# Attention's scale of q: sums of squares as rows through memory instead of columns straight from TensorE

## The chip, the cores and the metric

The kernel runs on one core of one Trainium2 chip. The metric is the device time of one execution in microseconds (us), as the median of several. Five engines work side by side: TensorE (PE, with its weight loads as PEld), VectorE (DVE), ScalarE (ACT), GpSimd (POOL) and SyncE (SP), which here issues all DMAs.

## The reference

A network of four layers over 16 meta tokens and 1024 tokens of width 1024, batch 1, fp32: sliding-window attention, mLSTM, HGRN2, attention again. Every layer adds its branch to x. What the change touches is the norm of q, and of k, ahead of the scores (16 heads of 64 for q, 4 for k):

```python
def rmsnorm(x, g):
    xf = x.astype(jnp.float32)
    y = xf * lax.rsqrt(jnp.mean(xf * xf, axis=-1, keepdims=True) + EPS)
    return (y * g.astype(jnp.float32)).astype(x.dtype)
...
def attention_branch(u, w_in, q_gain, k_gain, sinks, w_out, valid, pos):
    q, k, v, z = _split(u @ w_in, (A_W, A_KVW, A_KVW, A_W))
    q = rope(rmsnorm(q.reshape(bsz, lp, A_HEADS, A_HD), q_gain), pos)
    k = rope(rmsnorm(k.reshape(bsz, lp, A_KV, A_HD), k_gain), pos)
    ...
    o = sliding_window_attention(q, k, v, sinks, valid)
    return (o * jax.nn.silu(z.astype(jnp.float32))).astype(u.dtype) @ w_out
```

The window is 128 tokens; a softmax with one sink per head closes the scores.

## The kernel before

Activations lie transposed: features on the 128 partitions, tokens along the free axis. The 1040 tokens form chunks of 400, 384 and 256 columns (384, 384 and 256 for q, z and the output of the last layer, which needs no meta tokens there). Blocks of tokens are 16 (the meta tokens, block 0) and then 128 each; chunk 0 has blocks 0 to 3, chunk 1 has 4 to 6, chunk 2 has 7 and 8. Large products are split into high and low parts and made as three products each (`uh,wh`, `ul,wh`, `uh,wl`, line 232, eight feature tiles to an output tile). A weight tile arrives as two raw halves (`wr`, L208; two raw buffers in all), is cast on ACT (`wh`, L196), and DVE takes the difference (`wl`, L197).

**q.** The 16 heads of q make eight tiles t of 128 features, two heads to a tile. For each tile and chunk n the product is brought from PSUM by ACT twice (L576 with the gain, L577 squared, `sq`, one of six temporary tiles `t`). Then come steps at set delays behind the projection, in ns of PE's planned time (`D_Q` = 2000, 3000, 4000, 6000; `D_Q0` for the first two tiles of the first layer):

- `factors`: the load of the cosines and sines of a chunk (`cs`, L586, one buffer);
- `stat_q` (L590 to L610): sums of squares of each token and head. For every block one product (L599) with the block of squares as weights (128 × 128) and two mask columns as the moving side, so that the sums come out as two columns per block, with tokens on the partitions. In the first layer DVE adds the row's epsilon column (L604) and ACT makes Ln (L607) and Exp (L610); in the last layer ACT makes Ln from PSUM (L609) and Exp. The result is the tile `rq`, 1/rms of each token and head as columns, 128 × 2 per block;
- `rope` (L626 to L628), on q itself and on a copy of it with halves exchanged, which four DMAs bring (L570, issued as soon as q is out of PSUM);
- the split of q into high and low (`qs`, L528 and L529).

The scale is not put on q. The score step `S_step` takes it: PE makes the scores of two tiles (`pm`, L728 and L729), DVE multiplies by `rq`, masks and takes the minimum in one operation (L736), ACT makes Exp with the sum (L739), DVE the reciprocal (L741), POOL the product with it (L742). Then PE transposes (L757), ACT and DVE split (L759, L760), and PE multiplies by v (L775).

k's norm has its own step (`stat`, L616 a product with a 128-column mask as weights). The mLSTM layer writes rows of its gates to memory (`rowsd`, L927) and reads them back (`rw`, L992).

**Order.** PE's order is written by hand: a list of steps, each with a planned cost, woven by shares (`weave`) with events put in at their delays (`spread`, `chain`). The planned cost of a step moves the steps behind it against others; PE then runs in that order. ACT, DVE, POOL and SP are ordered by the tile scheduler. SP runs its DMAs in program order: one that waits holds all behind it.

Of the kernel before, what the change touches and what calls it, by code (L numbers as in the profile page):

```python
# [9 lines left out]
F32 = mybir.dt.float32  # L10
F32R = mybir.dt.float32r
AF = mybir.ActivationFunctionType
ALU = mybir.AluOpType
PSUM = bass.MemoryType.PSUM

P = 128
D = 1024
KT = D // P
NMETA = 16
# [7 lines left out]
CHUNK_BLOCKS = [(0, 1, 2, 3), (4, 5, 6), (7, 8)]  # L27


def blk(b):  # L30
    return (0, NMETA) if b == 0 else (NMETA + P * (b - 1), P)
# [24 lines left out]
MM = 1.0 / 2.4  # L56
# [58 lines left out]
def hybrid_kernel(ctx: ExitStack, tc: tile.TileContext, ins, out, layers=(0, 1, 2, 3)):  # L115
    nc = tc.nc
    v, s, g, pe, sp = nc.vector, nc.scalar, nc.gpsimd, nc.tensor, nc.sync
# [6 lines left out]
    dram = ctx.enter_context(tc.tile_pool(name="dram", bufs=1, space=bass.MemoryType.DRAM))  # L124
# [4 lines left out]
    def nm(x):  # L129
        ctr[0] += 1  # L130
        return f"{x}{ctr[0]}"
# [16 lines left out]
    def psum(tag, bufs):  # L148
        return ps.tile([P, 512], F32, tag="p", name=nm(tag), bufs=8)
# [4 lines left out]
    def psa():  # L154
        return psum("pa", 1)
# [8 lines left out]
    eps, one = consts[:, 0:1], consts[:, 1:2]  # L164
# [316 lines left out]
    def layer_a(i, j, first, last, fin, scale=None):  # L481
        win, wout = ins["a_win"][j], ins["a_wout"][j]
        chunks = LAST_CHUNKS if last else CHUNKS
        R = {}
# [72 lines left out]
        def qk_proj(src, gcol, work, fsplit, ch, t=None, fetched=False):  # L557
# [23 lines left out]
            def finish(n, c0, cn):  # L581
# [7 lines left out]
                def stat_q():  # L589

                    sq = late[n][1]
                    nb = len(CHUNK_BLOCKS[n])
                    R["rq", t, n] = rq = R["mix"].tile([P, 2 * nb], F32, tag=f"rq{n}", name=nm("rq"), bufs=4)
                    st = psa()
                    for k, b in enumerate(CHUNK_BLOCKS[n]):
                        if last and b == 0:
                            continue
                        q0 = blk(b)[0] - c0
                        pe.matmul(st[:, 2 * k : 2 * k + 2], sq[:, q0 : q0 + P], R["masks"][:, 0:P:64], start=True, stop=True)  # L599
                    z = slice(2 if last and n == 0 else 0, 2 * nb)  # L600
                    if first:
                        b0 = CHUNK_BLOCKS[n][0]
                        e = scale.ecol[:, b0 : b0 + nb].rearrange("p (k c) -> p k c", c=1).to_broadcast([P, nb, 2])
                        v.scalar_tensor_tensor(rq.rearrange("p (k c) -> p k c", c=2),  # L604
                                               st[:, z].rearrange("p (k c) -> p k c", c=2), 1.0 / 64, e,
                                               op0=ALU.mult, op1=ALU.add)
                        s.activation(rq, rq, AF.Ln)  # L607
                    else:
                        s.activation(rq[:, z], st[:, z], AF.Ln, bias=eps, scale=1.0 / 64)  # L609
                    s.activation(rq[:, z], rq[:, z], AF.Exp, scale=-0.5)  # L610

                def stat():
                    factors()
# [18 lines left out]
                turn = fsplit(lambda: late[n][0], n, c0, cn)  # L632
                if t is not None:
                    d = D_Q0 if first and t < 2 else D_Q
                    return [(d[0], [0.0, factors, None]), (d[1], [108 * len(CHUNK_BLOCKS[n]), stat_q, None]),
                            (d[2], [0.0, rope, None]), (d[3], turn)]
                d = D_K1 if fetched else D_K0 if scaled else D_K
                return [(d[0], [(8 if scaled else 4) * cn * MM, stat, None]), (d[1], [0.0, rope, None]), (d[2], turn)]

# [216 lines left out]
        for i in range(3, 12):  # L856
            for t in (2 * (i // 3), 2 * (i // 3) + 1):
                at = [id(z) for z in body]
                q, k = (at.index(id(z)) if id(z) in at else -1
                        for z in (order["q", t, i % 3], order["S", i // 3 - 1, i % 3]))  # L860
# [663 lines left out]
    for pos, i in enumerate(layers):  # L1524
# [16 lines left out]
        if tail is not None:  # L1541
            oa0, ob0 = tail
            first, seq = outs([oa0[0], ob0[0], oa0[1], oa0[2], ob0[1], ob0[2]])
# [6 lines left out]
            for n, start, end in ((2, t_b, t_b + h0 + h1), (1, t_a, t_b + h0), (0, 0.0, t_b)):  # L1550
                d, share = NORM_AT[n]
# [17 lines left out]
    first, seq = outs(tail[0] + tail[1])  # L1569
# [12 lines left out]
    ahead, k = 0.0, 0  # L1582
# [120 lines left out]
```

## Time and profile before

| | |
|---|---|
| time, median of 3 runs | 2576.55 us (2576.28 to 2578.90) |
| profiled execution | 2579.45 us, span 2577.7 us |
| granted clock, mean | 0.997 |
| first attention layer's mixers | about 22 to 488 us of the span |
| mLSTM and HGRN2 layers | about 488 to 2125 us |
| last attention layer's mixers | about 2125 to 2522 us |
| `stat_q` steps | 48 (24 in each attention layer) |
| products on L599 | 136 (two passes each) |

In a row of the trace, the first two numbers are its start from the start of the span and its duration (us); then engine, line, operation, what is written and read, and shapes. Idle time of the engine just ahead of it stands in brackets, with what ended it. A group of rows by line gives the least, median and largest duration in ns. PE's matmuls overlap: a product's duration is longer than the pitch from one to the next.

### The profile page before, as it was taken

The page shows a single profiled execution, that of the slowest core. Times are in us where ns is not written, and L with a number is a line of the kernel's source. Part 1 is how long each engine was busy: PE and PEld are TensorE (multiplying, and loading weights), DVE is VectorE, ACT ScalarE, POOL GpSimd, SP SyncE. Part 2 cuts the span into 40 slices and gives each one's busy share as a digit, 9 for nine tenths or more (in the row PEclk, how much of TensorE's full clock was granted, in tenths as well). Part 3 has the DMA queues.
Part 4 walks back from the last instruction along what each step waited for, and adds up shares of the span by engine and source line. Part 5 has one row for each costly group of instructions (what it writes and reads, how often), then busy time and mean ns, then how long its engine had stood idle before and what let it go on. Part 6 is the DMA issues. An engine that isn't in the chain of part 4 may idle for free. (4 is left out here: it accounts for less than half of the span.)

```text
span 2577.7 us, 55464 instructions
## 1 busy us (share of the span) xinstructions
PE 2530.0 (98%) x20614; PEld 2481.4 (96%) x20614; DVE 2028.8 (79%) x5602; ACT 1748.3 (68%) x4699; POOL 248.8 (10%) x572
## 2 busy tenths in 40 slices
PE   9999999999999999999999999999999999999999
PEld 8898989999999999999999999999999998999999
DVE  7896898786767676767676788988878988887896
ACT  8866766576565656565675758877676857867772
POOL 0321231000000000000000000110010000321320
PEclk9999999999999999999999999999999999999999
DMA  5223212022232212121221111111111013212112
GB/s 156 65 66 86 58 54 70 25 58 50 50 47 53 46 46 51 48 48 51 48 53 52 55 44 34 35 35 35 43 34 40 29 52 93 65 47 78 56 42 78
DMA packets 103345, 140.27 MB, mean 54 GB/s; under 512 B 15370, under 2 KB 58515, under 8 KB 103075
## 3 DMA queue, kind: packets, MB, share of 16 engines
q1 hardware_dynamic: 103074, 136.73, 19.7%
q8 instruction: 162, 2.65, 0.4%
q14 instruction: 109, 0.88, 0.1%
HBM read 121.83 MB, written 4.27 MB: 49 GB/s over the span
## 5 line engine op out<-in xcount | busy, mean ns | idle before, releaser
L232 PE MATMUL pj<-uh,wh 128*128 128x384 f32 (+2 forms) x2688 | 903.2, 336 | 6.7 <-ACT uh L402 6.2
L232 PE MATMUL pj<-ul,wh 128*128 128x384 f32 (+2 forms) x2688 | 864.8, 322 | 0.3
L232 PE MATMUL pj<-uh,wl 128*128 128x384 f32 (+2 forms) x2688 | 864.3, 322 | 0.0
L232 PEld LDWEIGHTS pj<-uh,wh 128*128 128x128 f32 x2688 | 507.9, 189 | 14.8 <-ACT uh L402 6.2
L232 PEld LDWEIGHTS pj<-ul,wh 128*128 128x128 f32 x2688 | 508.5, 189 | 4.7 <-DVE ul L197 0.9
L232 PEld LDWEIGHTS pj<-uh,wl 128*128 128x128 f32 x2688 | 507.5, 189 | 0.0
L197 DVE TENSOR_TENSOR wl<-wr,wh 128x512 fp32r<-128x512 f32 (+1 forms) x338 | 233.3, 702 | 74.6 <-ACT wh L196 71.3
L196 ACT CAST wh<-wr 128x512 fp32r<-128x512 f32 (+1 forms) x338 | 203.6, 613 | 93.5 <-PE pj L327 31.7
L327 PE MATMUL pj<-yh,wh 128*128 128x384 f32 (+2 forms) x768 | 252.9, 329 | 10.1 <-DVE x L330 8.3
L330 DVE TENSOR_TENSOR x<-x,pj 128x384 f32<-128x384 f32 (+2 forms) x480 | 233.8, 507 | 34.5 <-PE pj L327 33.2
L327 PE MATMUL pj<-yh,wl 128*128 128x384 f32 (+2 forms) x768 | 245.9, 320 | 0.0
L327 PE MATMUL pj<-yl,wh 128*128 128x384 f32 (+2 forms) x768 | 245.8, 320 | 0.0
L282 PE MATMUL pj<-wh,uh 128*128 128x256 f32 (+1 forms) x768 | 221.9, 289 | 0.0
L282 PE MATMUL pj<-wl,uh 128*128 128x256 f32 (+1 forms) x768 | 216.2, 282 | 0.0
L282 PE MATMUL pj<-wh,ul 128*128 128x256 f32 (+1 forms) x768 | 215.7, 281 | 0.0
L739 ACT ACTIVATE Sm<-Sm,s 128x257 f32<-128x257 f32 (+2 forms) x272 | 131.1, 483 | 88.9 <-DVE s L736 86.0
L742 POOL TENSOR_TENSOR Sm<-Sm,s 128x512 f32<-128x512 f32 (+2 forms) x136 | 139.3, 1025 | 402.5 <-DVE s L741 381.1
L459 ACT ACTIVATE t<-t 128x384 f32<-128x384 f32 (+2 forms) x240 | 118.2, 492 | 67.6 <-DVE t L458 65.8
L196 ACT CAST yh<-r 128x384 fp32r<-128x384 f32 (+2 forms) x120 | 56.8, 479 | 151.1 <-PE pj L327 135.6
L327 PEld LDWEIGHTS pj<-yh,wh 128*128 128x128 f32 x768 | 144.5, 188 | 14.3 <-DVE x L330 10.4
L282 PEld LDWEIGHTS pj<-wh,uh 128*128 128x128 f32 x768 | 144.6, 188 | 0.6
L282 PEld LDWEIGHTS pj<-wl,uh 128*128 128x128 f32 x768 | 144.8, 189 | 0.3
(332 smaller groups left out, 5684.2 us busy)
## 6 DMA issues: line engine op xcount, KB each, us to landing
wr<-in_b_win SPq DMA_DIRECT2D x124, 256.0 KB, 2.9
wr<-in_a_win SPq DMA_DIRECT2D x80, 256.0 KB, 2.8
wr<-in_c_win SPq DMA_DIRECT2D x64, 256.0 KB, 2.8
wr<-in_a_wout SPq DMA_DIRECT2D x32, 256.0 KB, 2.9
rw<-rowsd SPq DMA_DIRECT2D x64, 128.0 KB, 4.4
wr<-in_b_wout SPq DMA_DIRECT2D x32, 256.0 KB, 2.8
t<-t SPq DMA_DIRECT2D x100, 48.0 KB, 1.9
cs<-in_rope SPq DMA_DIRECT2D x11, 400.0 KB, 3.3
```

The costliest lines, as they stand in the source:

```text
L196: s.copy(h, src)
L197: v.tensor_tensor(l, src, h.bitcast(F32), op=ALU.subtract)
L232: pe.matmul(acc[:, :cn], a[:, k, :], b[:, k, c0 : c0 + cn], start=(k == 0 and i == 0), stop=(k == KT - 1 and i == 2))
L282: pe.matmul(acc[:cn, :nc], a[:, k, c0 : c0 + cn], m[:, kk, :], start=(k == 0 and j == 0), stop=(k == KT - 1 and j == 2))
L327: pe.matmul(acc[:, :cn], a[:, k, mc], b, start=(k == 0 and i == 0), stop=(k == 1 and i == 2))
L330: v.tensor_tensor(x[:, m, c0 : c0 + cn], x[:, m, c0 : c0 + cn], acc[:, :cn], op=ALU.add)
L459: s.activation(a[:, :cn], a[:, :cn], AF.Exp)
L739: s.activation(Sm[:nq, u, : nk + 1], Sm[:nq, u, : nk + 1], AF.Exp, scale=-1.0, bias=st[:nq, u : u + 1], accum_out=den[:nq, u : u + 1])
L742: g.tensor_tensor(Sm[:nq, :, :nk], Sm[:nq, :, :nk], den[:nq].rearrange("p (u c) -> p u c", c=1).to_broadcast([nq, 2, nk]), op=ALU.mult)
```

## The change

`stat_q` is cut in two. The first step makes one product for the whole chunk, with the two mask columns as weights (128 × 2) and all squares of the chunk as the moving side; ACT brings the two rows of sums out of PSUM (the scaled sums in the first layer, their Ln in the last) into the first two partitions of the tile of squares, and SP writes them to memory (`sd`). The second step, `rows_q`, comes behind `rope`, at least 1700 ns of planned time after the first: two DMAs (one a head) read the rows back as columns of `rq`, 4 bytes a piece, and for chunk 0 of the first layer a small third one the meta tokens, after POOL has set those columns to 1. DVE's addition and ACT's Ln (first layer) and Exp (both) are made on the columns as before. In all there are 48 writes and 104 reads more. The planned cost of the step goes from 108 ns a block (432, 324, 216) to 4 × columns / 2.4 (667, 640, 427).

```diff
@@ -589,25 +589,39 @@
                 def stat_q():
 
                     sq = late[n][1]
+                    st = psa()
+                    pe.matmul(st[:2, :cn], R["masks"][:, 0:P:64], sq, start=True, stop=True)
+                    if first:
+                        s.activation(sq[0:2], st[:2, :cn], AF.Identity, scale=1.0 / 64)
+                    else:
+                        s.activation(sq[0:2], st[:2, :cn], AF.Ln, bias=eps[0:2], scale=1.0 / 64)
+                    R["sd", t, n] = dram.tile([2, cn], F32, name=nm("sd"))
+                    sp.dma_start(R["sd", t, n], sq[0:2])
+
+                def rows_q():
+
                     nb = len(CHUNK_BLOCKS[n])
                     R["rq", t, n] = rq = R["mix"].tile([P, 2 * nb], F32, tag=f"rq{n}", name=nm("rq"), bufs=4)
-                    st = psa()
-                    for k, b in enumerate(CHUNK_BLOCKS[n]):
-                        if last and b == 0:
-                            continue
-                        q0 = blk(b)[0] - c0
-                        pe.matmul(st[:, 2 * k : 2 * k + 2], sq[:, q0 : q0 + P], R["masks"][:, 0:P:64], start=True, stop=True)
-                    z = slice(2 if last and n == 0 else 0, 2 * nb)
+                    d = R["sd", t, n]
+                    k = 0
+                    if n == 0:
+                        k = 1
+                        if not last:
+                            g.memset(rq[:, 0:2], 1.0)
+                            with nc.allow_non_contiguous_dma(reason="scale of each row"):
+                                sp.dma_start(rq[:NMETA, 0:2], d[:, :NMETA].rearrange("h t -> t h"))
+                    o = blk(CHUNK_BLOCKS[n][k])[0] - c0
+                    with nc.allow_non_contiguous_dma(reason="scale of each row"):
+                        for hh in range(2):
+                            sp.dma_start(rq[:, 2 * k + hh :: 2], d[hh, o:cn].rearrange("(k t) -> t k", t=P))
+                    z = rq[:, 2 if last and n == 0 else 0 :]
                     if first:
                         b0 = CHUNK_BLOCKS[n][0]
                         e = scale.ecol[:, b0 : b0 + nb].rearrange("p (k c) -> p k c", c=1).to_broadcast([P, nb, 2])
-                        v.scalar_tensor_tensor(rq.rearrange("p (k c) -> p k c", c=2),
-                                               st[:, z].rearrange("p (k c) -> p k c", c=2), 1.0 / 64, e,
-                                               op0=ALU.mult, op1=ALU.add)
+                        y = rq.rearrange("p (k c) -> p k c", c=2)
+                        v.tensor_tensor(y, y, e, op=ALU.add)
                         s.activation(rq, rq, AF.Ln)
-                    else:
-                        s.activation(rq[:, z], st[:, z], AF.Ln, bias=eps, scale=1.0 / 64)
-                    s.activation(rq[:, z], rq[:, z], AF.Exp, scale=-0.5)
+                    s.activation(z, z, AF.Exp, scale=-0.5)
 
                 def stat():
                     factors()
@@ -632,8 +646,8 @@
                 turn = fsplit(lambda: late[n][0], n, c0, cn)
                 if t is not None:
                     d = D_Q0 if first and t < 2 else D_Q
-                    return [(d[0], [0.0, factors, None]), (d[1], [108 * len(CHUNK_BLOCKS[n]), stat_q, None]),
-                            (d[2], [0.0, rope, None]), (d[3], turn)]
+                    return [(d[0], [0.0, factors, None]), (d[1], [4 * cn * MM, stat_q, None]),
+                            (d[2], [0.0, rope, None]), (max(d[3], d[1] + 1700.0), [0.0, rows_q, None]), (d[3], turn)]
                 d = D_K1 if fetched else D_K0 if scaled else D_K
                 return [(d[0], [(8 if scaled else 4) * cn * MM, stat, None]), (d[1], [0.0, rope, None]), (d[2], turn)]
 
```


With the lines that came in, the same code stands 14 lines lower behind the change: L736 is L750 in the changed kernel, L728 is L742, L692 is L706, L626 to L628 are L640 to L642. Lines up to L586 keep their numbers. Numbers at the end of names tell buffers apart and differ between the two kernels.

**PE**, first layer, the step of a q tile's chunk 0 among scores of the first pair (`qs` are split q, `t_1111` and `t_1133` the squares). Before:

```order
L728 MATMUL pm_1201<-r_488,qs_530 128x256
L729 MATMUL pm_1201<-r_489,qs_530 128x256
L728 MATMUL pm_1201<-r_488,qs_622 128x256
L729 MATMUL pm_1201<-r_489,qs_622 128x256
L599 MATMUL pa_1217<-masks_186,t_1111 128x2 x4
L775 MATMUL po_1134<-Ph_1147,v_833 128x2x128
L775 MATMUL po_1134<-Pl_1148,v_833 128x2x128
```

Now:

```order
L742 MATMUL pm_1223<-r_496,qs_538 128x256
L743 MATMUL pm_1223<-r_497,qs_538 128x256
L742 MATMUL pm_1223<-r_496,qs_633 128x256
L743 MATMUL pm_1223<-r_497,qs_633 128x256
L593 MATMUL pa_1238<-t_1133,masks_186 2x400
L789 MATMUL po_1156<-Ph_1169,v_849 128x2x128
L789 MATMUL po_1156<-Pl_1170,v_849 128x2x128
```

The step stands at the same place among the same neighbours; four products became one.

**SP**, last layer, where q tile 0 ends and q tile 1 is made, just ahead of the first scores (`wr` raw halves of weights, `cs` the rope factors, `t<-t` the exchanged halves of q). Before:

```order
L586 DMA cs_30564<-in_rope 128x2x256
L208 DMA wr_30768<-in_a_win 128x512
L208 DMA wr_30772<-in_a_win 128x512
L570 DMA t_30607<-t_30605 32x384 x4
L586 DMA cs_30660<-in_rope 128x2x400
L208 DMA wr_30874<-in_a_win 128x512
L208 DMA wr_30878<-in_a_win 128x512
L570 DMA t_30676<-t_30674 32x384 x4
L570 DMA t_30720<-t_30718 32x256 x4
L586 DMA cs_30727<-in_rope 128x2x384
L208 DMA wr_31412<-in_a_win 128x512
L208 DMA wr_31416<-in_a_win 128x512
```

Now, from the rope load of tile 1's chunk 0 (`cs_30660` before, `cs_30751` here) on; `wr_30863` and `wr_30867` are the halves that were `wr_30768` and `wr_30772`:

```order
L586 DMA cs_30751<-in_rope 128x2x400
L208 DMA wr_30863<-in_a_win 128x512
L616 DMA rq_30753<-sd_30709 128x2x1 x2
L570 DMA t_30771<-t_30769 32x384 x4
L599 DMA sd_30781<-t_30698 2x384
L586 DMA cs_30820<-in_rope 128x2x384
L599 DMA sd_30842<-t_30770 2x384
L570 DMA t_30813<-t_30811 32x256 x4
L616 DMA rq_30822<-sd_30781 128x3x1 x2
L586 DMA cs_30853<-in_rope 128x2x256
L208 DMA wr_30867<-in_a_win 128x512
```

The first half stands behind the rope load of chunk 0 where it stood ahead of it; the second behind the rope loads of chunks 0, 1 and 2 of tile 1, where it stood ahead of all three. Between them are writes to `sd` and reads into `rq`, and the halves of the next weight tile (`wr_30874` and `wr_30878` before) follow behind a further write and reads. The rope load of chunk 1 (`cs_30820`, before `cs_30727`) went ahead of chunk 2's exchanged halves (`t_30813`, before `t_30720`).

**DVE**, at the first scores of the last layer (the `ISA` rows are L736, now L750, the fused scale, mask and minimum). Before:

```order
L197 TENSOR_TENSOR wl_30873<-wr_30878,wh_30872 128x512
L692 TENSOR_TENSOR v_30817<-pt_30812,v_30817 16x128
L626 TENSOR_TENSOR t_30674<-t_30674,cs_30727 128x384
L627 TENSOR_TENSOR t_30676<-t_30676,cs_30727 128x384
L692 TENSOR_TENSOR v_30821<-pt_30812,v_30821 128x128
L628 TENSOR_TENSOR t_30674<-t_30674,t_30676 128x384
L692 TENSOR_TENSOR v_30824<-pt_30812,v_30824 128x128
L736 ISA Sm_30851,s_30852<-pm_30850,masks_30212,cons_30214,rq_30421 128x144
```

Now:

```order
L706 TENSOR_TENSOR v_30915<-pt_30910,v_30915 16x128
L706 TENSOR_TENSOR v_30919<-pt_30910,v_30919 128x128
L640 TENSOR_TENSOR t_30811<-t_30811,cs_30853 128x256
L641 TENSOR_TENSOR t_30813<-t_30813,cs_30853 128x256
L706 TENSOR_TENSOR v_30922<-pt_30910,v_30922 128x128
L642 TENSOR_TENSOR t_30811<-t_30811,t_30813 128x256
L197 TENSOR_TENSOR wl_30862<-wr_30867,wh_30861 128x512
L706 TENSOR_TENSOR v_30925<-pt_30910,v_30925 128x128
L750 ISA Sm_30953,s_30954<-pm_30952,masks_30300,cons_30302,rq_30542 128x144
```

The rope of tile 1's chunk 2 and the difference of that second half of a weight stand ahead of the first score step; before, the rope of chunk 1 was the last one ahead of it, and the difference (then `wr_30772`) stood seventeen rows further up.

## The prediction

> **What bounds the kernel now.** I read the page's first part, the granted clock, the busy time by stretches of the run, the waits of PE, and then single rows around the change. The page first (engine, busy us, share of the span, instructions), then three stretches: the mixers of the first attention layer, those of the last, and the start of the last layer's scores. Columns of the stretches: window, length, busy us of PE, PEld, DVE, ACT and POOL, granted clock, DMA share, GB/s.
>
> ```profile
> PE 2530.0 (98%) x20614; PEld 2481.4 (96%) x20614; DVE 2028.8 (79%) x5602; ACT 1748.3 (68%) x4699; POOL 248.8 (10%) x572
> ```
> ```profile
> 22.00:488.00 466.00, 449.87 (x3047) 433.43 (x3046) 399.99 (x1048) 330.87 (x926) 97.86 (x186) 0.99 0.23 66
> ...
> 2125.00:2522.00 397.00, 386.36 (x2671) 377.93 (x2670) 339.89 (x860) 292.05 (x797) 85.53 (x127) 1.00 0.22 64
> ...
> 2186.00:2206.00 20.00, 17.37 (x129) 16.86 (x128) 16.86 (x56) 15.37 (x48) 6.74 (x12) 1.00 0.23 68
> ```
>
> TensorE is the bound: 98% busy at a granted clock of 0.99 to 1.00. It idles 466.00 − 449.87 = 16.1 us in the first stretch and 10.6 us in the second. What the other engines do costs time only where it lengthens such an idle piece, and PE's order is fixed by hand, so a stall in it is not filled by later work. The largest group of stalls is the transpose of the softmax'd scores, which waits for POOL (total us, times, longest):
>
> ```profile
> PE pt L757 <- POOL Sm L742: 9.8, 10, 2.2
> ```
>
> **The change on PE.** Removed: 8 steps with four blocks, 24 with three, 16 with two, each block a product of 128 weight columns (the squares) and 2 moving columns. Added: 48 products with 2 weight columns and 400, 384 or 256 moving ones. I price a step by what it delays: from its start to the start of the second product behind it, less that product's ordinary pitch (0.175 us for 384 or 400 columns).
>
> ```profile
> 101.98 0.95 PE L599 MATMUL pa<-masks,t 128*128 128x2 f32 x8
> 102.79 0.42 PE L232 MATMUL pj<-uh,wh 128*128 128x384 f32 x1
> 103.05 0.34 PE L232 MATMUL pj<-ul,wh 128*128 128x384 f32 x1
> ```
> ```profile
> 57.32 0.50 PE L599 MATMUL pa<-masks,t 128*128 128x2 f32 x4
> 57.68 0.43 PE L232 MATMUL pj<-uh,wh 128*128 128x400 f32 x1
> 57.95 0.34 PE L232 MATMUL pj<-ul,wh 128*128 128x400 f32 x1
> ```
> ```profile
> 2152.49 0.81 PE L616 MATMUL pa<-r,masks 128*128 128x384 f32 x2
> 2152.84 0.63 PE L232 MATMUL pj<-uh,wh 128*128 128x384 f32 x1
> 2153.31 0.34 PE L232 MATMUL pj<-ul,wh 128*128 128x384 f32 x1
> ...
> 2162.69 0.59 PE L616 MATMUL pa<-r,masks 128*128 128x256 f32 x2
> 2162.94 0.53 PE L232 MATMUL pj<-uh,wh 128*128 128x384 f32 x1
> 2163.30 0.34 PE L232 MATMUL pj<-ul,wh 128*128 128x384 f32 x1
> ```
>
> Four blocks: 103.05 − 101.98 − 0.175 = 0.895 us; two: 0.63 − 0.175 = 0.455; so 0.224 a block, 0.67 for three. For the new product the nearest rows are k's own sums (L616): two passes over as many columns, but 128 weight columns. They give 0.82 − 0.175 = 0.645 for 384 columns and 0.61 − 0.175 = 0.435 for 256, hence about 0.67 for 400. The term is 8 × (0.67 − 0.895) + 24 × (0.645 − 0.67) + 16 × (0.435 − 0.455) = −1.8 − 0.6 − 0.3, about **−2.6 us**. No row shows 2 weight columns with a wide moving side. If such a product cost 0.08 more, as much as a block's pair of passes can vary, the term would be +1.2. A shorter weight load would bring at most 48 × 0.05 = −2.4 more: loads run beside products already (PEld 96% under PE 98%). I take −2.6, from the row nearest in form.
>
> **The way through memory.** A column tile rq is now ready after a row operation on ACT, a write, a dependent read and an Exp. How soon it is wanted:
>
> ```profile
> 31.38 0.29 ACT L610 ACTIVATE rq<-rq 128x8 f32<-128x8 f32 x2
> ```
> ```profile
> 65.03 0.28 DVE L736 CUSTOM_DVE_ANT_0 Sm<-pm,masks,cons 16x16 f32<-16x16 f32 x1
> ```
> ```profile
> 2177.68 0.21 ACT L610 ACTIVATE rq<-rq 128x6 f32<-128x6 f32 x1
> ```
> ```profile
> 2187.05 0.43 DVE L736 CUSTOM_DVE_ANT_0 Sm<-pm,masks,cons 128x144 f32<-128x144 f32 x1
> ...
> 2187.40 0.42 DVE L736 CUSTOM_DVE_ANT_0 Sm<-pm,masks,cons 128x144 f32<-128x144 f32 x1
> ```
>
> In the first layer 65.03 − 31.38, over 33 us, lie between; at the start of the last layer's scores, the tightest place, 2187.40 − 2177.68 = 9.7 us. The mLSTM layer makes such a trip already, a row to memory and back:
>
> ```profile
> 530.71 0.30 SPq L927 DMA_DIRECT2D rowsd<-r  x1
> 532.86 1.41 SPq L992 DMA_DIRECT2D rw<-rowsd  x3
> ```
> ```profile
> rw<-rowsd SPq DMA_DIRECT2D x64, 128.0 KB, 4.4
> ...
> rw<-rowsd SPq DMA_DIRECT2D x8, 16.0 KB, 2.6
> ```
>
> The read goes out 2.15 us after the write, and lands 2.6 us later for 16 KB, 4.4 for 128 KB. The new reads carry 1 to 1.5 KB in 4-byte pieces, a form that no row shows; between those two rows I take 2.6, the smaller in bytes. The trip is then about 2.2 + 0.5 + 2.6 + 0.2 = 5.5 us, 7.3 with the longer landing: under 9.7, so its latency alone costs **nothing**. The cover would be gone from 9.7 us on, microsecond for microsecond, at one place; elsewhere far later.
>
> A rule that speaks against this: the Trainium skill, page "DMA: Bandwidth & Descriptors", section "Rules for kernel authors", says that a last dimension that is not contiguous becomes one descriptor per element, and that a transpose by a rearranged access pattern is 19 times worse than the hardware's own. By that, a landing of 2.6 us would be nearer 49, an estimate from that page. No run here shows such pieces; it stands as a rival below.
>
> **ACT and DVE.** On ACT the row operation comes in. Nearest rows (count, then ns least, median, most), one row of 400 from PSUM, and the column form which the last layer drops:
>
> ```profile
> L441 ACT ACTIVATE r<-pa x3: 357/463/477, 24.0 to 54.8; 1x400 f32<-1x400 f32 x1, 1x384 f32<-1x384 f32 x1, 1x256 f32<-1x256 f32 x1
> ```
> ```profile
> L609 ACT ACTIVATE rq<-pa,consts x24: 243/266/293, 2150.0 to 2434.3; 128x6 f32<-128x6 f32 x16, 128x4 f32<-128x4 f32 x8
> ```
>
> First layer 24 × 0.46 = 11.1, last 24 × (0.46 − 0.27) = 4.7: 15.8 us more of ACT, on an engine 71 to 74% busy in these stretches. DVE swaps one small operation for another in the first layer, at nothing. PE idles 3.5% and 2.7% of the two stretches, 13% at the start of the last layer's scores; I let a tenth of ACT's extra reach PE: **+1.6 us**, bounds 0 (all hidden) and 3.2 (a fifth). The waits for the reads stand in ACT's and DVE's order (Exp in both layers, the add in the first), with casts for uh, qs and weights queued behind them; the step comes 1.7 us of PE's time after the statistic at least, and the scheduler puts them later still, so I price them inside that bound.
>
> **SP and the start of the last layer's scores.** 152 DMAs come in on SP's queue in program order; a write waits for ACT and a read for its write: 0.3 for the write, up to 1.85 of waiting, 2 × 0.47 for the reads (1.41 for three above), some 3 us a step. SP has room for that, since its longest waits are those of weight loads for a free buffer (us, times, longest):
>
> ```profile
> SPq L208 <- DVE wl L197: 1057.5, 228, 39.3
> ```
>
> It has none where a weight that is soon wanted stands behind such a wait, as at the start of the last layer's scores:
>
> ```profile
> 2166.74 0.94 SPq L208 DMA_DIRECT2D wr<-in_a_win  x2
> ...
> 2173.60 1.52 SPq L208 DMA_DIRECT2D wr<-in_a_win  x2
> ...
> 2181.25 0.58 SPq L586 DMA_DIRECT2D cs<-in_rope  x1
> ...
> 2186.11 4.24 SPq L586 DMA_DIRECT2D cs<-in_rope  x2
> ```
> ```profile
> 2174.05 0.68 DVE L197 TENSOR_TENSOR wl<-wr,wh 128x512 fp32r<-128x512 f32 x1
> ...
> 2178.17 0.56 DVE L628 TENSOR_TENSOR t<-t,t 128x384 f32<-128x384 f32 x1
> ...
> 2186.21 0.55 DVE L628 TENSOR_TENSOR t<-t,t 128x384 f32<-128x384 f32 x1
> ```
> ```profile
> wr<-in_a_win SPq DMA_DIRECT2D x80, 256.0 KB, 2.8
> ```
> ```profile
> L196 ACT CAST wh<-wr 128x512 fp32r<-128x512 f32 (+1 forms) x338 | 203.6, 613 | 93.5 <-PE pj L327 31.7
> ```
> ```profile
> 2190.82 0.65 PE L757 MATMUL pt<-ident,Sm 128*128 128x128 f32 x4 [1.92 <-POOL Sm L742]
> ```
>
> The second half of the weight that went out at about 2167.2 stands now behind the rope load of chunk 2 (SP's rows above). That load waits for DVE to finish the rope of chunk 1 (2186.76 before). Chunk 1's own load, behind rotations at 2181.25 before, stands ahead of those of chunk 2 now and can go when chunk 0's rope has ended, at 2178.17 + 0.56, about 2178.8. That is 2.4 us earlier, so chunk 1's rope ends near 2184.3. Then: rope load 2184.5, weight half issued 2185.3, landed 2.8 later, cast on ACT 0.6, difference on DVE 0.7 (the rows above): 2189.4. (The rope of chunk 2, ahead of the scores now as well, has its load 0.8 us earlier and is done by then.) On DVE that difference, at 2174.05 before, stands now just ahead of the first score step, before at 2187.05. So the scores start **+2.4 us** later, and PE, which waits 1.92 us for this chain at 2190.82 already, waits all of it. If chunk 1's rope ends earlier the term goes to 0; if it ends as before, and a read's wait of 1.2 comes in too, 2.4 + 2.5 + 1.2 = +6.
>
> **Sum.** −2.6 + 2.4 + 1.6 = +1.4 us. The profiled execution took 2579.45 us (span 2577.7 and 1.75 around it), 2.9 above the median; the difference is carried to the median: 2576.55 + 1.4, about **2578.0 us**. What this measurement tells from no change is about 0.2%, 5.2 us: 2571.4 to 2581.7.
>
> **Rivals.**
> Faster: the late start doesn't come, and the freed waits pay. DVE's L604 waited in order for PE 5.3 us in all, such as
>
> ```profile
> 46.97 0.16 DVE L604 SCALAR_TENSOR_TENSOR rq<-pa,scale 128x6 f32<-128x6 f32 x1 [2.39 <-PE pa L599]
> ```
>
> If a third of the 9.8 us that PE waits for scores goes with them, −2.6 − 3.3 gives 2570.7. Against it: those 9.8 us wait on the chain DVE, ACT, POOL, which the change doesn't shorten. 0.14.
>
> Slower: SP's queue is the price. Weights and rope loads stand behind writes and reads that wait, at the start of the last layer's scores and also at the first's. It decides once the weight half's difference ends past 2189.4: each microsecond further is one of PE's. With +6 there, 3.2 from ACT and a tenth of a microsecond for each of 48 trips, −2.6 + 6 + 3.2 + 4.8 = +11.4: 2588. For it: four queues get waits in order; against it: SP's long idle. 0.33.
>
> Far slower: a read in 4-byte pieces lands after 49 us. Both starts would wait, 49 − 9.7 and 49 − 33 more, some 55 us: 2632. The page named above says so. Against it in this case: reads of 256 rows land in 2.6 and 4.4 us as their bytes differ, so the number of pieces isn't what counts. 0.05.
>
> That the change does nothing to the time is inside the forecast.
>
> **How the numbers follow.** Forecast (0 to +3.5 around the sum, two weak terms cancelling) 0.48, all of it within 0.2%; faster rival 0.14; slower rival 0.33; far slower 0.05. So faster 0.14, same 0.48, slower 0.38. The range takes the faster rival's 2570.7 and the slower's 2588 as its ends, and leaves out the far slower case and the edges of the others.
>
> **What would show it.** PE's busy time falls by 2 to 3 us; the new product's group delays by 0.65 for 384 columns. The reads of rq land in about 2.6 us. SP issues the weight half near 2185 and PE's first wait at the scores grows from 1.9 to about 4.3 us. I am wrong if landings pass 5 us, if ACT's row operation takes over 0.6 us, or if PE's idle time grows at the first layer's start.

## The result, and the profile after

The changed kernel takes **2603.02 us** (median, 2601.87 to 2605.17) against 2576.70 beside it: 26.3 us more, a ratio of 1.010, interval 1.0087 to 1.0112. The forecast was 2578.0, the range ended at 2588.0. It is slower by five times what this measurement can tell from no change.

The runs of one kernel scatter with the granted clock: of the kernel before, those beside the experiments took 2578.5 us on average at a clock of 0.997 and 2573.0 at 0.999, so that a few microseconds of any one pair of runs below are the clock's.

The page's first part of the changed kernel, and the stretch of the first layer's mixers, with the columns as in the prediction:

```profile
span 2603.3 us, 55436 instructions
...
PE 2546.5 (98%) x20438; PEld 2461.6 (95%) x20438; DVE 2037.3 (78%) x5602; ACT 1764.9 (68%) x4723; POOL 244.3 (9%) x580
```
```profile
22.00:488.00 466.00, 445.84 (x2849) 410.34 (x2848) 392.23 (x1016) 330.19 (x926) 94.41 (x178) 0.98 0.25 64
```

The span grew by 25.6 us. PE is still 98% busy, yet its busy time grew by 16.5 us, although it has fewer products (20438 records for 20614), and its idle time (span less busy) by 9.1, from 47.7 to 56.8. So two things are to be found: what makes PE busy for longer, and what it waits for.

**Busy for longer, first: the new product.** PE around one product of 384 columns and one of 256:

```profile
2175.35 0.28 PE L232 MATMUL pj<-uh,wl 128*128 128x256 f32 x1
2175.56 0.81 PE L593 MATMUL pa<-t,masks 128*2 128x384 f32 x2
2176.30 0.39 PE L232 MATMUL pj<-uh,wh 128*128 128x256 f32 x1
2176.52 0.28 PE L232 MATMUL pj<-ul,wh 128*128 128x256 f32 x1
2176.64 0.28 PE L232 MATMUL pj<-uh,wl 128*128 128x256 f32 x1
...
2256.72 0.34 PE L232 MATMUL pj<-uh,wl 128*128 128x384 f32 x1
2256.99 0.59 PE L593 MATMUL pa<-t,masks 128*2 128x256 f32 x2
2257.52 0.44 PE L232 MATMUL pj<-uh,wh 128*128 128x384 f32 x1
2257.80 0.34 PE L232 MATMUL pj<-ul,wh 128*128 128x384 f32 x1
```

From the start of the product to the second one behind it, less that one's pitch (0.12 for 256 columns, 0.175 for 384): 2176.52 − 2175.56 − 0.12 = 0.84 us, and 0.81 − 0.175 = 0.635. The product ahead is also held: 0.21 and 0.27 us to the next start where its pitch is 0.12 and 0.175, so 0.09 more each. That makes 0.93 for 384 columns and 0.72 for 256, where three blocks cost 0.67 and two 0.455: +0.26 each, 40 times, about **+10.5 us**. The eight of 400 columns come to 0.96 in the trace where four blocks cost 0.895, half a microsecond more in all. The product that I took for its like (L616, 128 weight columns) lets the next one start after 0.35 us; this one holds it for 0.74.

**Busy for longer, second: the granted clock.** Its mean fell from 0.997 to 0.994, which is 2603.3 × 0.006 − 2577.7 × 0.003, some 8 us of lost clock. A part of that falls where PE stands still. Where PE works, half of its busy time at the half clock is lost: 14.0 us in this trace and 6.8 in the one before, so about **+7 us**. It is lost in a few pieces, each behind idle time of PE. Two pieces in slices of 10 us, and 2 us of the first:

```profile
70.00:80.00 10.00, 6.37 (x41) 5.71 (x39) 4.94 (x16) 5.01 (x17) 0.66 (x4) 0.84 0.45 137
80.00:90.00 10.00, 9.44 (x48) 9.38 (x49) 7.67 (x27) 7.10 (x25) 3.26 (x7) 0.68 0.18 61
2370.00:2380.00 10.00, 9.14 (x37) 8.84 (x38) 5.66 (x11) 7.79 (x18) 0.00 (x0) 0.67 0.43 133
```
```profile
82.00:84.00 2.00, 2.00 (x9) 1.99 (x8) 1.71 (x4) 1.84 (x6) 0.82 (x2) 0.50 0.08 18
```

Within such a slice the clock is whole or half (0.50 in the last row). A slice of 10 us at 0.67 has lost 3.3 us. The Trainium skill, page "TensorE: Matmul & The Clock Gate", section "Why this matters for your kernels", says that pauses of PE over some 3 us bring back the half clock. The trace agrees on the half, and at 2370.86 (below) it comes behind a pause of 3.05 us. On the length the measurement differs: in the kernel before, a pause of 2.24 us was enough, with 3.2 us lost in its slice:

```profile
243.80 1.22 PE L616 MATMUL pa<-t,masks 128*128 128x256 f32 x2 [2.24 <-ACT t L577]
```
```profile
240.00:250.00 10.00, 7.76 (x27) 5.95 (x25) 4.17 (x9) 6.74 (x16) 0.00 (x0) 0.68 0.32 95
```

Nor does a pause of that length always do it: the one of 2.24 us that ends at 2207.61 in the changed kernel (below) lost nothing, the slices 2200 to 2210 and 2210 to 2220 both stand at 1.00.

**Waits.** At the start of the first layer's scores PE waits 3.81 and 2.85 us, where it waited 2.17 and 1.19 at the same rows before. Before, and now:

```profile
67.86 0.39 PE L757 MATMUL pt<-ident,Sm 128*16 128x128 f32 x2 [2.17 <-POOL Sm L742]
73.25 0.28 PE L775 MATMUL po<-Ph,v 128*128 128x32 f32 x1 [1.19 <-ACT Ph L759]
```
```profile
69.63 0.60 PE L771 MATMUL pt<-ident,Sm 128*16 128x128 f32 x2 [3.81 <-POOL Sm L756]
77.53 0.28 PE L789 MATMUL po<-Ph,v 128*128 128x32 f32 x1 [2.85 <-ACT Ph L773]
```

Ahead of the first, ACT and DVE run in another order. ACT's cast for the split of q, which stood at 61.55, comes at 63.77, behind a copy that waits for PE, and DVE's split and score steps come after it. Before, and now:

```profile
61.55 0.84 ACT L528 CAST qs<-t 64x256 fp32r<-64x256 f32 x2
```
```profile
63.77 0.81 ACT L528 CAST qs<-t 64x256 fp32r<-64x256 f32 x2
```

In the second, ACT's cast of a weight that lands late stands ahead of the copy that PE waits for (line 773, the first rows below; before, line 759, the last row, which ran ahead of the next cast at 76.69):

```profile
76.79 0.62 ACT L196 CAST wh<-wr 128x512 fp32r<-128x512 f32 x1 [1.95 <-DMA wr<-in_a_win]
77.31 0.25 ACT L773 CAST Ph<-pt 16x32 fp32r<-16x32 f32 x2
```
```profile
73.03 0.25 ACT L759 CAST Ph<-pt 16x32 fp32r<-16x32 f32 x2
```

In the last layer, where k's second tile is made, SP's reads into `rq` stand ahead of a rope load and, behind it, of the exchanged halves (`t<-t`) that DVE's rope waits for. DVE's rope is late, so are the temporary tiles that it frees, so is ACT's copy of k out of PSUM (L576, which waited 0.62 us at this place before), and PE waits. SP, DVE, ACT and PE there, and the copy before:

```profile
2362.39 2.12 SPq L616 DMA_DIRECT2D rq<-sd  x4
2364.61 0.41 SPq L586 DMA_DIRECT2D cs<-in_rope  x1
```
```profile
2368.11 0.57 DVE L640 TENSOR_TENSOR t<-t,cs 128x400 f32<-128x400 f32 x1 [1.43 <-DMA t<-t]
```
```profile
2365.24 0.20 ACT L624 ACTIVATE rq<-rq 128x4 f32<-128x4 f32 x1 [1.43 <-DMA rq<-sd]
...
2369.82 0.47 ACT L576 ACTIVATE t<-pj,cons 128x256 f32<-128x256 f32 x1 [2.39 <-DVE t L642]
```
```profile
2370.86 1.22 PE L630 MATMUL pa<-t,masks 128*128 128x256 f32 x2 [3.05 <-ACT t L577]
```
```profile
2345.94 0.47 ACT L576 ACTIVATE t<-pj,cons 128x256 f32<-128x256 f32 x1 [0.62 <-DVE t L628]
```

And the place that the prediction worked out, the start of the last layer's scores:

```profile
2200.47 0.47 SPq L208 DMA_DIRECT2D wr<-in_a_win  x1
```
```profile
2204.13 0.69 DVE L197 TENSOR_TENSOR wl<-wr,wh 128x512 fp32r<-128x512 f32 x1
...
2204.94 0.42 DVE L750 CUSTOM_DVE_ANT_0 Sm<-pm,masks,cons 128x144 f32<-128x144 f32 x1
...
2206.41 0.17 DVE L755 RECIPROCAL s<-s 128x2 f32<-128x2 f32 x1
```
```profile
2207.61 0.66 PE L771 MATMUL pt<-ident,Sm 128*128 128x128 f32 x4 [2.24 <-POOL Sm L756]
```

### The profile page after: what moved, and what is told of

Read it like the earlier page. It is cut to its first block, busy times and chain, and to the rows that moved or that the text cites. A ratio compares the mean times of both kernels' runs of the same rounds, so it can differ in the third digit from the quotient of the medians.

```text
span 2603.3 us, 55436 instructions
## 1 busy us (share of the span) xinstructions
PE 2546.5 (98%) x20438; PEld 2461.6 (95%) x20438; DVE 2037.3 (78%) x5602; ACT 1764.9 (68%) x4723; POOL 244.3 (9%) x580
## 4 chain that ended last, share of the span: by engine, by line
PE 63%; DVE 12%; ACT 9%; DMA 2%; issue 2%; SPq 1%; POOL 0%; DVEq 0%; ACTq 0%; POOLq 0%
PE pj L232 29%; PE pj L327 15%; PE pj L282 9%; PE po L1022 2%; DVE wl L197 1%; DVE Sm L750 1%; ACT Sm L753 1%; PE po L789 1%; PE pt L771 1%; ACT wh L196 1%; ACT X L1341 1%; DVE Pl L774 1%; PE pa L1022 1%; DVE t L458 1%; PE pt L1113 1%
## 5 line engine op out<-in xcount | busy, mean ns | idle before, releaser
L327 PEld LDWEIGHTS pj<-yl,wh 128*128 128x128 f32 x768 | 144.9, 189 | 2.1 <-DVE yl L197 1.7
```

The source lines that it names most:

```text
L327: pe.matmul(acc[:, :cn], a[:, k, mc], b, start=(k == 0 and i == 0), stop=(k == 1 and i == 2))
```

## The experiments

The change has three parts: the form of the product, the trip through memory, and the planned cost, which shifts PE's order. Each was undone or done alone. Where the sums can't come back as columns, the kernel leaves the scale out: the same operations run, but `rq` holds other numbers (e3, e4, e7, e9, e12, e15 to e18). "Before" is always the run beside it on the same chip. PE's idle time is the page's span less its busy time.

**e1: 128 weight columns**

```diff
-pe.matmul(st[:2, :cn], R["masks"][:, 0:P:64], sq, start=True, stop=True)
+pe.matmul(st[:, :cn], R["masks"][:, 0:P], sq, start=True, stop=True)
...
-sp.dma_start(R["sd", t, n], sq[0:2])
+sp.dma_start(R["sd", t, n], sq[0:P:64])
```

> The changed kernel with one edit: the row product has all 128 mask columns as weights instead of 2, ACT's row operation runs over 128 partitions instead of 2, and the write takes partitions 0 and 64. Theory: a product with 2 weight columns holds PE up, 0.88 us for 384 columns together with 0.09 us ahead of it, where k's own sums (L616 before) with 128 columns take 0.645. With 128 columns it should take 0.645 again: 8 x 0.22 + 24 x 0.23 + 16 x 0.28, about 11 us less than the changed kernel's 2603, so 2592. Rival: the row product costs that much for another reason (the place, the kind of neighbour), and nothing changes: 2603.

Measured: 2598.79 against 2576.19 (1.0091, interval 1.0077 to 1.0104). The product itself did what was expected. PE in this kernel:

```profile
2166.64 0.28 PE L232 MATMUL pj<-uh,wl 128*128 128x256 f32 x1
2166.76 0.81 PE L593 MATMUL pa<-t,masks 128*128 128x384 f32 x2
2167.11 0.58 PE L232 MATMUL pj<-uh,wh 128*128 128x256 f32 x1
2167.53 0.28 PE L232 MATMUL pj<-ul,wh 128*128 128x256 f32 x1
```

0.77 − 0.12 = 0.65 us, the predicted 0.645, and nothing ahead of it. PE's busy time falls by 13 us to 2533.5, but its idle time grows from 56.8 to 62.7, so only some 4 us of the 13 arrive, and as the two intervals overlap, even these are not certain. What PE saves there it waits for elsewhere.

**e2: the four forms of the weights in one kernel**

```diff
+c, u = ((0, 2), (63, 2), (48, 32), (32, 64))[t // 2]
+w = R["masks"][:, 0:P:64] if t < 2 else R["masks"][:, c : c + u]
+pe.matmul(st[:u, :cn], w, sq, start=True, stop=True)
```

> The changed kernel with the weights of the row product in four forms, by pair of q tiles: 2 columns 64 apart (as in the change), 2 columns side by side, 32, 64. It is for the duration of each group on PE. If the distance of the columns counts, 2 side by side take 0.65 for 384 moving columns instead of 0.79 and 0.09 ahead; if the number counts, 2 side by side are as slow as 2 apart, and 32 or 64 are at 0.645 or between.

Measured (2603.56, one run): the next product starts 0.74 us behind that of 384 columns with 2 weight columns apart, 0.74 with 2 side by side, 0.76 with 32 and 0.79 with 64, and the product ahead is held by 0.09 in all of them. With 64:

```profile
2444.62 0.86 PE L595 MATMUL pa<-t,masks 128*64 128x384 f32 x2
2445.41 0.39 PE L232 MATMUL pj<-uh,wh 128*128 128x256 f32 x1
```

The distance doesn't count, and of the forms tried only all 128 columns let the neighbours overlap.

**e3 and e4: before's products with the trip; the new product without the trip**

```diff
 e3: products of the blocks as before, and
-s.activation(sq[0:2], st[:2, :cn], AF.Identity, scale=1.0 / 64)
+s.activation(sq[0:2], sq[0:2], AF.Identity, scale=1.0 / 64)
 e4: no writes and reads, no rows_q; in stat_q, behind the row operation,
+v.scalar_tensor_tensor(rq..., sq[:, z]..., 1.0 / 64, e, op0=ALU.mult, op1=ALU.add)
+s.activation(rq, rq, AF.Ln)
+s.activation(rq[:, z], rq[:, z], AF.Exp, scale=-0.5)
```

> The changed kernel with before's products: blocks as weights, two columns out of each. The row operation of ACT runs on two rows of squares in their own tile instead of the sums, so rq holds no scale; writes, reads, Ln, Exp and the planned cost stay. Theory: the products are worth 10 us (8 x 0 + 24 x 0.26 + 16 x 0.26), the trip through memory with its waits and the halved clock behind them 16: 2593. Rival one: the trip costs nothing and all comes from the products: 2577. Rival two: all comes from the trip: 2603.

> The changed kernel without the trip: the row product and ACT's row operation stay, nothing is written or read, and the column operations run at once on columns of the tile of squares (so rq holds no scale). Theory: the products' 10 us stay, the stalls and their clock go: 2587. Rival: products alone explain it: 2603. Other rival, all from the trip: 2577.

Measured: e3 2589.26 against 2576.19 (1.0056, 1.0043 to 1.0069), e4 2587.24 (1.0039, 1.0025 to 1.0052). 13.1 and 11.0 us: both rivals fall, each half is real. The pages show them as different things:

```profile
span 2585.9 us, 55807 instructions
...
PE 2530.7 (98%) x20614; PEld 2484.0 (96%) x20614; DVE 2031.2 (79%) x5602; ACT 1769.2 (68%) x4723; POOL 246.6 (10%) x580
```
```profile
span 2587.2 us, 55149 instructions
...
PE 2538.6 (98%) x20438; PEld 2455.9 (95%) x20438; DVE 2031.1 (79%) x5602; ACT 1767.0 (68%) x4747; POOL 249.6 (10%) x572
```

With the trip alone (first) PE's busy time is as before and its idle time 55.2; with the product alone (second) busy time is up 8.6 and idle time at 48.6, nearly as before. ACT has its row operations in both, and both have the change's planned cost.

**e5, e6, e7: what in the trip costs**

```diff
 e5: sp.dma_start of sd and rq becomes g.dma_start
 e6: the reads and column operations later
-(max(d[3], d[1] + 1700.0), [0.0, rows_q, None]), (d[3], turn)]
+(d[3], turn), (d[1] + 6000.0, [0.0, rows_q, None])]
 e7: e4 with the writes, and the reads into a tile that nothing reads
+ru = R["mix"].tile([P, 8], F32, tag="ru", name=nm("ru"), bufs=2)[:, : 2 * nb]
```

> The changed kernel with its 152 writes and reads issued by POOL instead of SP. The trip with before's products cost 13 us. Theory S: they come from SP's queue, where rope loads and weights stand behind writes and reads that wait; then SP is as before and some 10 of the 13 go: 2593, less what POOL loses, since its product of the scores (L756) now stands behind the same waits. Theory A: they come from the waits of ACT and DVE for the reads (Exp and the addition in order ahead of casts); those stay, and the time stays at 2603.

> The changed kernel with the reads and the column operations 6000 ns of planned time behind the row product instead of 1700 or 3000, behind the split of q. The reads then find their write done and SP waits less, and ACT and DVE find the reads landed. Both theories (SP's queue; in-order waits of ACT and DVE) say that most of the 13 us of the trip go: 2593. If only the number of DMAs on SP counts, or the work itself, the time stays near 2603.

> The kernel without the trip (e4, 2587) with the writes and reads put back on SP at their places, but into a tile that nothing uses; the column operations run at once on columns of squares, so ACT and DVE never wait for a read (rq holds no scale). Theory S (SP's queue): 2587 + 12, about 2599. Theory A (waits of ACT and DVE): 2587.

Measured against 2575.86: e5 2617.93 (1.0162, 1.0147 to 1.0178), e6 2593.74 (1.0071, 1.0058 to 1.0084), e7 2594.90 (1.0080, 1.0066 to 1.0094). e7 stands between the theories: 8 us above e4, from which it differs by DMAs on SP that nobody waits for, and 7 below the whole change, which would be the waits for the reads. e6 agrees that the place of the reads counts: with the reads later, 8 us go. The first and the last of the three places above show the same, in e7 (first fence) and e6 (second):

```profile
70.03 0.39 PE L776 MATMUL pt<-ident,Sm 128*16 128x128 f32 x2 [3.66 <-POOL Sm L761]
...
2361.03 1.22 PE L635 MATMUL pa<-t,masks 128*128 128x256 f32 x2 [3.01 <-ACT t L577]
```
```profile
68.34 0.39 PE L771 MATMUL pt<-ident,Sm 128*16 128x128 f32 x2 [2.03 <-POOL Sm L756]
...
2359.45 0.70 PE L630 MATMUL pa<-t,masks 128*128 128x256 f32 x2 [0.84 <-ACT t L577]
```

Without the trip (e4) PE waits 1.80 and 0.75 us there, with before's products and the trip (e3) 4.34 and 3.52. So among kernels that differ in the trip alone these two waits come and go with the reads at their early places, whether anything waits for the reads or not. They can come without them too: kernels with 128 weight columns and no trip (e9, e12, e16 and e17, below) wait 2.6 to 3.3 us at the first place, and e14, with later reads, 2.69 at the second. So whether SP's queue itself makes them, or the order that the scheduler gives the other engines around these DMAs, is not told apart. The wait at 77 us doesn't follow the reads: it is 2.90 in e6 and 0.87 in e7.

e5 made it worse. It also shows the landing of the reads, which SP's queue gives no row of. POOL's groups and its reads' landing:

```profile
L616 POOL DMA_DIRECT2D rq<-sd x96 | 72.8, 760 | 48.0 <-DMA sd<-t 42.0 <-issue 4.8 <-PE po L789 0.9
```
```profile
rq<-sd POOLq DMA_DIRECT2D x64, 1.5 KB, 2.6
rq<-sd POOLq DMA_DIRECT2D x32, 1.0 KB, 2.8
```

On POOL an issue takes 0.76 us and the reads wait 42 us in all for their writes, ahead of the product of the scores, on the chain that PE waits for: its waits there grow from 11.4 us in the changed kernel to 16.5. DVE and ACT wait 18.6 and 16.7 us for the reads, 3.2 and 2.9 in the changed kernel; which of these costs made the 15 us more is not separated. The reads land in 2.6 and 2.8 us.

**e11 and e13: the planned cost**

```diff
 e11, on the changed kernel (e13, on the kernel before, the other way round)
-(d[1], [4 * cn * MM, stat_q, None]),
+(d[1], [108 * len(CHUNK_BLOCKS[n]), stat_q, None]),
```

> The changed kernel with the planned cost of the step as before, 108 ns a block. If the planned costs (which place PE's steps against each other) play a part, the time moves by more than 3 us; theory: they don't, 2603.

> The kernel before with the planned cost of the step alone changed, 4 x columns / 2.4 instead of 108 a block; every instruction stays, PE's order moves. If the order is a part of the loss: +8 to +10, 2585. If not: 2576.

Measured: e11 2592.55 against 2575.87 (1.0070, 1.0057 to 1.0082), e13 2580.28 against 2576.36 (1.0022, 1.0012 to 1.0032). The expectation for e11 was wrong: undoing the planned cost takes 8 to 10 us off the changed kernel (by the ratios and by the medians), while doing it alone adds 4 to 6 to the one before. It is a part of the change with a price. The first rows of PE that stand otherwise, at the first scores of whole blocks (`pm` scores, `pj` a projection). Before:

```order
L757 MATMUL pt_1007<-ident,Sm_909 128x128 x4
L728 MATMUL pm_1016<-r_488,qs_375 128x256
L729 MATMUL pm_1016<-r_489,qs_375 128x256
L728 MATMUL pm_1016<-r_488,qs_381 128x256
L729 MATMUL pm_1016<-r_489,qs_381 128x256
L232 MATMUL pj_1031<-uh,wh_796 128x400
```

In e13:

```order
L757 MATMUL pt_1007<-ident,Sm_909 128x128 x4
L232 MATMUL pj_1016<-uh,wh_796 128x400
L232 MATMUL pj_1016<-ul,wh_796 128x400
L232 MATMUL pj_1016<-uh,wl_797 128x400
L232 MATMUL pj_1016<-uh,wh_796 128x400
L232 MATMUL pj_1016<-ul,wh_796 128x400
L232 MATMUL pj_1016<-uh,wl_797 128x400
L728 MATMUL pm_1023<-r_488,qs_375 128x256
```

The scores moved behind a piece of a projection, and so on through both attention layers. How this costs time is not followed further here. The wait at 77 us is one place: 2.85 us in the changed kernel, 0.19 in e11.

**e8, e10, e14: everything that was found cheap, together.** 128 weight columns and later reads (e8: 6000, e10: 9000), and in e14 the old planned cost as well.

> The changed kernel with 128 weight columns (as e1) and the reads 6000 ns behind the row product (as e6). If the two costs add: e6 stood 17.9 us above before, of which some 10.3 were the product with 2 columns, and with 128 it is 3 below the blocks: 17.9 - 10.3 - 3, about +5, 2581. If a faster PE only waits the more for what is late (as e1, which gained 4 of 13), 2590.

> As e8 with the reads 9000 ns behind the row product. If the reads at 6000 ns still hold SP or ACT up, this is some microseconds faster than e8; if the scores now wait for rq instead, slower; if what is left comes from the DMAs' number on SP, the same.

> The trip with 128 weight columns, reads 6000 ns later and the planned cost as before: each of the three costs in its cheap form. Against e8 (2593) the order's 8 to 10 us go: 2584; against before, what is left is the DMAs on SP less the product's gain.

Measured: e8 2593.28 and e10 2593.53 against 2575.87 (1.0065, 1.0052 to 1.0078; 1.0062, 1.0048 to 1.0075), e14 2588.89 against 2576.36 (1.0059, 1.0045 to 1.0072). The costs don't add: e8 gained nothing over e6, though PE is busy for 9 us less (2531.6 for 2540.4), since it idles 5 us more (57.9 for 53.0). Reads later still (e10) change nothing. No version with the trip comes near the kernel before.

**e9, e12, e15 to e18: the product without the trip, part by part.** e9 and e12 have 128 weight columns and the row operation (new and old planned cost), e15 is e4 with the old planned cost. e16 is the kernel before with one line changed; e17 adds ACT's row operation in PSUM; e18 has the 2-column product in its place and no row operation.

```diff
 e16
-for k, b in enumerate(CHUNK_BLOCKS[n]):
-    ...
-    pe.matmul(st[:, 2 * k : 2 * k + 2], sq[:, q0 : q0 + P], R["masks"][:, 0:P:64], start=True, stop=True)
+pe.matmul(st[:, :cn], R["masks"][:, 0:P], sq, start=True, stop=True)
 e17, behind it
+s.activation(st[:2, :cn], st[:2, :cn], AF.Identity, scale=1.0 / 64)
```

> The kernel without the trip (e4) with 128 weight columns, so PE's part of the change alone, in its cheap form (rq holds no scale). The prediction's term, -2.6, should come out: 2573. If ACT's row operation costs what the prediction gave it (1.6): 2575. If the product's form is not what e4's 11 us were: 2587.

> No trip, 128 weight columns (e9, +9) with the planned cost as before. If e9's 9 us were the order, the product's -3 is left: 2573. If they were ACT's row operation, 2585 stays.

> No trip, 2 weight columns (e4, +11) with the planned cost as before. If e4's 11 us were the 2-column product: 2587. If they were the order: 2576. Both in part: 10 from the group durations on PE, 2586, with the order's share hidden behind it.

> The kernel before with one edit: one product with 128 weight columns in place of the blocks; the column operations read the same number of columns of it as before (so rq holds no scale). No row operation, tile of squares free after the product, planned cost as before. By the durations on PE: -3, 2573. If the product itself is what e12's 8 us are: 2584.

> As e16, with ACT's row operation put in, on the two rows in PSUM, ahead of the column operations. If the work on ACT is what e12's 8 us are: 2584. If it is the held tile of squares: as e16, 2573 to 2575 (the prediction gave ACT's work 1.6).

> The kernel before with the change's product alone, 2 weight columns; the column operations read columns of squares (so rq holds no scale), there is no row operation. By the durations on PE +10: 2586, as e15. If e15's 10 us were the row operation or the held tile: 2576.

| kernel | ratio to before, interval | PE busy | PE idle |
|---|---|---|---|
| before | 1 | 2530.0 | 47.7 |
| e9, 128 columns, row operation, new cost | 1.0029, 1.0017 to 1.0040 | 2527.7 | 55.4 |
| e12, 128 columns, row operation, old cost | 1.0042, 1.0029 to 1.0054 | 2529.6 | 53.4 |
| e16, 128 columns alone | 1.0048, 1.0032 to 1.0064 | 2531.7 | 52.9 |
| e17, 128 columns, row operation in PSUM | 1.0038, 1.0026 to 1.0050 | 2531.7 | 52.3 |
| e15, 2 columns, row operation, old cost | 1.0047, 1.0034 to 1.0059 | 2539.9 | 47.7 |
| e18, 2 columns alone | 1.0063, 1.0050 to 1.0075 | 2538.8 | 49.4 |

The 2-column product is clear: e15 adds 9.9 us to PE's busy time and nothing to its idle time, as the durations of its groups say. ACT's row operation costs nothing that shows: e17 is not slower than e16, nor e15 than e18. The 128-column product is not clear. It was expected to win 3 us (e9, e12, e16), and the four kernels with it stand 8 to 13 above before by their medians, with 5 to 8 us more of idle time on PE. The two right columns account for 7 of e16's 13 us, since the execution of before that was profiled, 2579.45, lies 5 us above the median beside e16, 2574.13; e16's runs were granted 0.995 to 0.998 of the clock, those of before beside it 0.997 to 0.999, some 5 us. At the start of the last layer's scores e16's PE waits 4.11 us where it waited 1.92 before, while on DVE the rope of chunk 2 (as in the changed kernel) and a split of q stand ahead of the first score step:

```profile
2188.11 0.40 DVE L624 TENSOR_TENSOR t<-t,t 128x256 f32<-128x256 f32 x1
...
2190.42 0.42 DVE L732 CUSTOM_DVE_ANT_0 Sm<-pm,masks,cons 128x144 f32<-128x144 f32 x1
```
```profile
2192.79 0.66 PE L753 MATMUL pt<-ident,Sm 128*128 128x128 f32 x4 [4.11 <-POOL Sm L738]
```

No work came in there; the tile scheduler put DVE's, ACT's and SP's rows in another order. That this order alone is the cause was not tried: it can't be held while a product is exchanged.

## Why the prediction was wrong, point by point

- **The product on PE, −2.6, was the main step that failed.** It measured +10.5, 13 of the 25 us between forecast and result. The three kernels with this product and without the trip stand 10 to 16 us above before (e15, e4, e18). L616 was taken as "the row nearest in form", with as many moving columns but 128 weight columns, and the missing 2-column row was bounded at 0.08 more each; it is 0.28 with what it holds up ahead. The bound was drawn from the spread of a familiar form, not from a reason why an unfamiliar one should be like it. With 128 columns (e1) the predicted 0.645 came out.
- **The planned cost** was described ahead of the prediction and priced nowhere in it. The place in PE's order that is shown ahead of the prediction had not moved; others had. Alone it costs 4 to 6 us, in the changed kernel 8 to 10.
- **The trip's latency** was right: the reads land in 2.6 and 2.8 us (e5), and no score step waits for `rq`. The rival by which they would take 49, after the Trainium skill's page "DMA: Bandwidth & Descriptors", section "Rules for kernel authors", did not come: on these transfers of 256 and 384 pieces the trace speaks against a factor of 19.
- **SP's queue at the start of the last layer's scores** went as worked out. The weight half was forecast for 2185.3, its difference on DVE to end at 2189.4, the scores to start there. They stand at 2200.47, 2204.13 + 0.69 and 2204.94, with PE 16.5 us late by then (its transpose ahead of these scores, L690, starts at 2200.30 for 2183.83): 2184.0, 2188.3 and 2188.4, a microsecond earlier than forecast. The scores start 1.4 us later than before against PE. But PE's wait grew only from 1.92 to 2.24, since DVE's reciprocal, which POOL's product waits for, now follows the score steps at once, where q's split and two steps of a rope stood between: 2206.41 for 2189.86, just PE's own 16.5 us. That "PE waits all of it" was the step that failed in this term: +2.4 measured +0.3.
- **The other places were left out.** The slower rival named this mechanism and the first layer's start, and its price of +11.4 was too small because it had the product at −2.6. With the measured product it comes to 24.5, near the 26.3, but partly by luck, since the +6 in it was for a place that gave 0.3. That PE's idle time grows at the first layer's start is one of the signs by which the prediction called itself wrong. The places where PE lost most, at 69, 77 and 2370 us, were not worked out: at 2370 SP's reads hold up a rope load, at 77 a weight lands late, at 69 ACT and DVE run in another order. With the waits for the reads it made 6 (e11 less e15) to 15 us (the change less e4), according to the order.
- **ACT's extra work, +1.6,** can't be told from nothing: e17, with the row operation, is not slower than e16, nor e15 than e18. What did cost time was ACT's order, a cast or a copy standing ahead of what PE waits for.
- **The clock** did not occur in the sum. Stalls of 2 to 4 us cost up to 3.3 us more by the half clock behind them, some 7 us in all.

Product +10.5, idle time +9.1 and clock +7 make 26.6 for the 25.6 of the span, each worked out by itself. What is not settled is how the idle time and the clock divide between trip and order: the experiments show them interact, from 0 to 10 us for the planned cost according to what else is in the kernel. Why the kernels with 128 weight columns and no trip idle more than before stays open too.

## What to carry to other kernels

Price a new product shape by a row of that shape: here the number of weight columns, not the work, decided whether its neighbours overlapped. Where one engine is 98% busy in an order written by hand, a planned cost is an edit like any other, and a stall of 2 us or more can be paid twice, once as a wait and once at half clock. A term that comes out right on one engine need not reach the span: with 128 weight columns the product cost what was forecast, and no kernel with it was faster than the one before. Work that is off the critical path is not free if it puts a waiting transfer into a queue that also brings weights.

## What the runs showed that was not expected

- A product with 2, 32 or 64 weight columns holds the next one for 0.74, 0.76 or 0.79 us at 384 moving columns, against 0.35 with 128, and its predecessor by 0.09 (e2, e1).
- Shorter work on PE hardly shortened the run: e1 cut 13 us of PE's busy time and gained 4, e8 cut 9 against e6 and gained nothing by the medians.
- The same small reads take 0.76 us of issue on POOL, against 0.46 us on SP (medians):

```profile
L616 SPq DMA_DIRECT2D rq<-sd x96: 359/460/1844, 39.7 to 2462.9; - x96
```
